# Hybrid encoder trunk on one core: w_out's first half loaded in pairs, some sums moved into the down-projection, x added sooner, sample's attention drawn in at other steps

## The chip, the cores and the metric

The kernel runs on one core of one Trainium2 chip. The metric is the device time of one launch in microseconds. The kernel before takes 1517.93 us, the median of three runs (1512.95 to 1520.29). Engines are named as in the profile: PE is TensorE, DVE VectorE, ACT ScalarE, POOL GpSimd, SP SyncE, which issues nearly all DMAs.

## The reference

One layer of an encoder trunk is run on two requests with shared weights: `x_prompt` (512 rows) and `x_sample` (1024 rows), each row 1024 wide, all float32.

```
def _trunk(x, ...):
    h = _rmsnorm(x, norm_attn_g);  z = h @ w_in                # 1024 -> 1792
    q, k, v, ca, cb = split(z)                                 # 8 heads, 2 kv heads, 512 conv channels
    a_out = _window_attn(q, k, v, bias, band, attn_sink)       # |q-k| <= 128, sink logit
    c = _dwconv(ca * sigmoid(cb), conv_dw_w, conv_dw_b)        # 31 taps
    c = silu(_layernorm(c, conv_ln_g, conv_ln_b))
    x = x + concat([a_out, c]) @ w_out                         # 1024 -> 1024
    h = _rmsnorm(x, norm_ffn_g)
    u = _dwconv(h @ w_up, ffn_dw_w, ffn_dw_b)                  # 1024 -> 5632, 3 taps
    x = x + (silu(u[:, :2816]) * u[:, 2816:]) @ w_down         # 2816 -> 1024
    return _rmsnorm(x, norm_final_g)
```

## The kernel before, in words

**Arithmetic.** Each float32 operand is split into a high part (a rounding copy on ACT) and a low part (a subtraction on POOL or DVE), and each product takes three matmuls: high by high, high by low, low by high. A usual matmul is 128x128 by 128x512. The large products of sample are done in blocks by Strassen's scheme in Winograd's form, seven products in place of eight, with sums and differences of blocks made beforehand.

**Tiles and slots.** SBUF is cut into slots by hand: 15 of 4096 bytes ("q"), 4 of 4352 ("c"), 61 of 2048 ("h"), 2 of 2304 ("d") and small ones. `sb.tile` takes the least slot that fits. PSUM banks are named a, u, b, c, later w (two banks wide) and t.

**Order.** The program's text is a plain sequence with Python generators drawn into it. `side` is a queue of generators, and `tick()`, called between matmuls, advances the first of them by `pace["rate"]` steps; `drain` runs a queue to its end. The text sets a priority. The build then orders the instructions of each engine by a simulated timeline, so a later instruction that is ready can go ahead of one that is not. In the last part (`by_hand`) PE keeps the order of the text, and in the down-projection SP does too. Each engine then runs its own list in order.

**Stages.**

1. The projection by w_in, chunk by chunk (L500, L289). In the later chunks the prompt's windowed attention runs as side work (`prompt_attention`).
2. `prompt_out`: w_out of the prompt. For each half `n` of its columns the eight chunks of 128 rows are loaded and split, and four blocks of 128 rows go through `out_half` (L770 to L772, 24 matmuls, a step after each 6). Then `make_h2` scales the rows by their norm and transposes them (L248): eight steps, each with four transposes, a scaled high part on ACT (L250) and a low part on DVE (L251). In front of it stand, for each block, the evacuation on DVE (L775), a sum of squares on ACT (L781), the power -1/2 on POOL (L138, L139) and the scaling on DVE (L828). A `while out` loop counts these steps in `n`, some 50 in all (2 x (1 + 4 + 16) + 8, if nothing has to be waited for). From step 19 on, every fourth (`SA` = 4) also takes one unit of sample's attention, `units_of_sample`: scores (L624, L628, L637), then values (L666, L668, L680, L690).
3. The prompt's up-projection and gate, 22 calls of `ffn_step`, each with 8 ticks at a rate of 0.55. The side work is `sample()`: the remaining units of sample's attention, then a wait for step 21 (`KW`), then loads of w_out's sixteen pieces of 128x512 (`load_wo`, L791, 256 KB each) with their splits (`split_wo`, L802 on ACT, L803 on DVE for two of four (`DW2` = 2) and on POOL for the others), then the conv norm of blocks 4 and 5 (`conv_norm`: transposes L729, statistics, L738, transposes L744, ACT, and the low part L754). Convolution steps of sample run as `late` work (L317, L318). At the end `drain(side)` puts all that is left into the text.
4. w_out of sample, blocks 4 to 11, through `out_blocks`, in the order (4,0), (4,1), (5,0), (5,1), ...: block, half.
5. Turning of rows into operands (L1079), then sample's up-projection: 22 steps `j`, each with seven products (`first` to `seventh`, L1148 to L1150). L1219 and L1237 are ACT's copies that seed a PSUM bank for the next product of a step. The prompt's gates are stored in DRAM, and `sums_of(p)` makes the sums that Winograd's form needs of them: two loads of 256 KB, four POOL steps (L966 to L969), two stores of 256 KB. There are eleven `p`; one is made at each even `j` from 2, and the last at `j` = 18.
6. The down-projection of both requests: 77 steps (i, p), seven products `i` in the order 1, 2, 5, 6, 7, 4, 3 with eleven `p` each (L1477 to L1479). `down_step(k)` loads (`load_next`), makes the operands of step k + 4 (`LEAD`; `operands` and `split_of`, L1036 and L1032 for the pairs, L1460 and L1032 for the prompt's part), and issues 12 or 18 matmuls. `evacuate` adds a finished product to the sums u, e, o11, o12 (L1029). `load_x1` and `with_x` load the residual x and add it to a sum (L1029 too, one of three parts on DVE, two on POOL).
7. The last product, i = 3, in a loop of its own over eleven `p`. Beside it, six blocks of rows that are complete are finished: `finish` sums squares on ACT (L1526), takes the power on POOL (L1548, L1549), scales on DVE (L1559) and on ACT and POOL (L1555, L1557) and stores. The last two groups of rows come at the end.

## Time and profile before

| what | value |
|---|---|
| median of three runs | 1517.93 us (1512.95 to 1520.29) |
| the profiled execution's own time | 1514.8 us |
| its span, first to last instruction | 1513.0 us |
| granted clock, mean | 0.992 |
| DMA over the span | 228.19 MB, mean 151 GB/s |
| w_out's matmuls (L770), prompt and sample | 280.4 to 744.0 us |
| prompt's and sample's w_in and the prompt's up-projection (L289) | 42.5 to 636.6 us |
| sample's up-projection (L1148) | 744.7 to 1191.6 us |
| down-projection (L1477) | 1178.2 to 1506.3 us |

Times in the profile are counted from the span's start. A row of a timeline gives start and duration in us, the engine, the line, the operation, what it writes and reads by the tiles' slot letters, its shape and count, and in brackets how long the engine was idle before it and what ended that. A row of the waits gives the total in us, how often, and the longest. A group's row gives busy us, the mean ns of one, and the engine's idle time in front. "PEclk" is the share of full speed that TensorE's clock was granted. Ends of matmuls are modelled, so pipelined matmuls overlap in the rows; the distance of their starts is what one costs.

### The profile page before, as it was taken

What the parts mean: (1) busy time and instruction counts of PE and PEld (TensorE: products, weight loads), DVE (VectorE), ACT (ScalarE), POOL (GpSimd) and SP (SyncE); (2) the same over time, 40 slices, a digit from 0 to 9 for tenths busy, and PEclk for the clock granted to TensorE, in tenths of its full rate; (3) what the DMA queues carried; (4) which work ended last, traced back from release to release, by engine and by line L of the source; (5) the groups of instructions that cost most, each with busy time, mean ns of one, the idle gap of its engine ahead of it and who ended that gap; (6) DMA issues with size and microseconds to landing.
All of it is one profiled execution on the core that took longest, in us unless ns stands there. A gap on an engine that the chain in (4) does not pass through costs nothing. (4 is left out here: it accounts for less than half of the span.)

```text
span 1513.0 us, 19880 instructions
## 1 busy us (share of the span) xinstructions
PE 1480.5 (98%) x6736; PEld 1216.5 (80%) x6736; DVE 1106.2 (73%) x1508; ACT 801.7 (53%) x1421; POOL 785.1 (52%) x691
## 2 busy tenths in 40 slices
PE   8999999999999999999999999999999999999997
PEld 7888788877888888778788788888888888888876
DVE  7877945648999895665767888888776855657865
ACT  6424455467777876653464445444454453443345
POOL 3454353356987875342436566565565211215666
PEclk9999999999999999999999999999999999999998
DMA  9455241843443444763124333333343473446744
GB/s 372 168 162 150 85 108 36 252 145 126 147 129 129 132 139 136 260 203 99 70 73 151 132 133 126 127 126 130 129 151 123 164 272 102 133 151 213 236 155 162
DMA packets 125201, 228.19 MB, mean 151 GB/s; under 512 B 20483, under 2 KB 45827, under 8 KB 124972
## 3 DMA queue, kind: packets, MB, share of 16 engines
q1 hardware_dynamic: 123564, 225.32, 45.4%
q10 hardware_dynamic: 1536, 1.61, 0.3%
q8 instruction: 53, 0.87, 0.2%
q14 instruction: 48, 0.39, 0.1%
HBM read 166.83 MB, written 61.10 MB: 151 GB/s over the span
## 5 line engine op out<-in xcount | busy, mean ns | idle before, releaser
L155 POOL TENSOR_TENSOR q<-q,q 128x1024 fp32r<-128x1024 f32 x66 | 158.6, 2406 | 76.2 <-ACT q L154 58.4
L1032 DVE TENSOR_TENSOR h<-h,h 128x512 fp32r<-128x512 f32 (+1 forms) x155 | 134.3, 891 | 82.9 <-ACT h L1036 36.4
L1032 POOL TENSOR_TENSOR q<-q,q 128x512 fp32r<-128x512 f32 x81 | 117.1, 1455 | 116.4 <-ACT q L1134 116.4
L1477 PE MATMUL w<-h,h 128*128 128x512 f32 x444 | 173.7, 391 | 1.3 <-ACT h L1460 0.8
L1479 PE MATMUL w<-h,h 128*128 128x512 f32 x436 | 170.1, 390 | 0.0
L1478 PE MATMUL w<-h,h 128*128 128x512 f32 x428 | 167.4, 391 | 2.8 <-DVE h L1032 2.8
L289 PE MATMUL u<-h,q 128*128 128x512 f32 x384 | 151.2, 395 | 0.3 <-DVE h L251 0.3
L291 PE MATMUL u<-h,q 128*128 128x512 f32 x384 | 150.4, 392 | 0.0
L290 PE MATMUL u<-h,q 128*128 128x512 f32 x384 | 150.2, 392 | 0.0
L1148 PE MATMUL w<-h,q 128*128 128x512 f32 x368 | 143.9, 391 | 2.9 <-ACT w L1237 2.6
L1150 PE MATMUL w<-h,q 128*128 128x512 f32 x368 | 143.7, 391 | 0.0
L1149 PE MATMUL w<-h,q 128*128 128x512 f32 x347 | 135.5, 390 | 0.0
L1032 POOL TENSOR_TENSOR h<-h,h 128x512 fp32r<-128x512 f32 (+1 forms) x36 | 48.5, 1348 | 161.9 <-ACT h L1460 109.6
L1036 ACT CAST h<-h 128x512 fp32r<-128x512 f32 x119 | 71.4, 620 | 109.3 <-DVE h L1032 43.6
L1477 PEld LDWEIGHTS w<-h,h 128*128 128x128 f32 x444 | 83.8, 189 | 19.7 <-ACT h L1460 1.2
L154 ACT CAST q<-q 128x1024 fp32r<-128x1024 f32 x66 | 69.1, 1049 | 54.5 <-PE u L290 31.1
L326 DVE SCALAR_TENSOR_TENSOR c<-d,cvw,c 128x512 f32<-128x512 f32 x128 | 95.9, 749 | 1.6
L1478 PEld LDWEIGHTS w<-h,h 128*128 128x128 f32 x428 | 80.7, 189 | 20.0 <-DVE h L1032 3.4
L1479 PEld LDWEIGHTS w<-h,h 128*128 128x128 f32 x436 | 82.1, 188 | 17.1
L1032 POOL TENSOR_TENSOR c<-q,c 128x512 fp32r<-128x512 f32 x46 | 72.5, 1586 | 41.8 <-ACT c L1134 41.8
L318 POOL TENSOR_TENSOR h<-h,h 128x512 f32<-128x512 f32 x62 | 80.5, 1300 | 17.9 <-ACT h L317 15.7
L1148 PEld LDWEIGHTS w<-h,q 128*128 128x128 f32 x368 | 69.1, 188 | 18.6 <-ACT w L1237 3.0
(455 smaller groups left out, 4010.9 us busy)
## 6 DMA issues: line engine op xcount, KB each, us to landing
q<-in_laid_w_up SPq DMA_DIRECT2D x88, 512.0 KB, 3.8
ga<-q SPq DMA_DIRECT2D x65, 256.0 KB, 2.2
h<-gap SPq DMA_DIRECT2D x57, 256.0 KB, 3.5
h<-ga SPq DMA_DIRECT2D x57, 256.0 KB, 3.2
h<-in_w_down SPq DMA_DIRECT2D x52, 256.0 KB, 3.3
q<-in_laid_w_in SPq DMA_DIRECT2D x22, 512.0 KB, 3.9
gap<-h SPq DMA_DIRECT2D x44, 256.0 KB, 2.8
q<-in_x_sample SPq DMA_DIRECT2D x15, 512.0 KB, 7.1
```

Of the source, the lines that this page charges most:

```text
L155: (nc.vector if dve else nc.gpsimd).tensor_tensor(lo[:], raw[:], hi[:].bitcast(F32), op=ALU.subtract)
L289: nc.tensor.matmul(out, whi[:, kc, :], hi[:], start=(kc == 0), stop=False)
L290: nc.tensor.matmul(out, whi[:, kc, :], lo[:], start=False, stop=False)
L291: nc.tensor.matmul(out, wlo[:, kc, :], hi[:], start=False, stop=(kc == KC - 1))
L326: nc.vector.scalar_tensor_tensor(acc[:], src(t), w(t), acc[:], op0=ALU.mult, op1=ALU.add)
L1032: (eng or nc.vector).tensor_tensor(out, a, b, op=ALU.subtract)
L1148: nc.tensor.matmul(out, whi[:, s], hi[:], start=(start and c == 0), stop=False, **go)
L1149: nc.tensor.matmul(out, whi[:, s], lo[:], start=False, stop=False, **go)
L1150: nc.tensor.matmul(out, wlo[:, s], hi[:], start=False, stop=(stop and c == 3), **go)
L1477: nc.tensor.matmul(out, sh[:, c], th[:], start=(p == 0 and not seeded), stop=False, **go)
L1478: nc.tensor.matmul(out, sh[:, c], tl[:], start=False, stop=False, **go)
L1479: nc.tensor.matmul(out, sl[:, c], th[:], start=False, stop=(p == NPAIR - 1), **go)
```

## The change

Seven things are changed.

- **Attention in the prompt's out-projection:** a unit of sample's attention is taken at every third step (`SA` = 3) while `n` is below 40 (`N2`), and at none of the later steps that occur (`SA2` = 99).
- **w_out of sample:** once step 16 (`KL`) of the prompt's up-projection is reached, the next unit of attention also issues the loads of the eight pieces of half 0, as four transfers of two pieces each. The wait for step 21 is gone. After the attention, the pieces of half 1 are loaded while half 0 is split; then comes the norm of block 4, then the splits of half 1, and after the last of them (`WN` = 7) the norm of block 5. Three of four low parts go to DVE (`DW2` = 3).
- **Order of the blocks:** the `drain` at the end of the prompt's up-projection is gone; the order is (4,0), (5,0), (4,1), (5,1), then as before, and each entry first advances the side work until its norm and its half of w_out are there.
- **Sums:** `sums_of` became a generator with stops between its steps, and its first store moved up two POOL steps. Sums 0 to 7 are made at `j` = 4, 6, ..., 18; sums 8, 9, 10 are drawn, one stop a step, into the down-projection from its step 2 on, ahead of that step's loads.
- **x:** the load of x for o12 moves from step 6 to step 4 of product 4; x is added to u at step 10, ahead of that product's evacuation, where before it was added behind it; all these steps now stand ahead of the evacuation.
- **Lead:** operands are made up to two steps further ahead from step 62 of the down-projection on, and six ahead (`LZ`), not four, in the last product, which also issues three loads a step (`LN`), not two.
- **Slots:** in the last product the two parts of a split share one q slot where one is free.

```diff
@@
 SCB, SCD = "aapa", "aaap"
-WOP, WOA, DW, DW2 = 1, 5, 2, 2
+WOP, WOA, DW, DW2 = 1, 5, 2, 3
 NE = 2
 YN = 2
 OB = "cbu"
 NW = 16
 BL = 9
-SA = 4
+SA, N2, SA2 = 3, 40, 99
+KL, WN = 16, 7
+LN = 3
+SUM_AT = (4, 6, 8, 10, 12, 14, 16, 18)
+XP = (2, 4, 4, 8, 8, 10)
+LZ = 6
 AP = 1
-KW = 21
 class Slots:
@@
         n += 1
         if n > 7:
             next(doubling, None)
-        if n % SA == 0 and n > 18:
+        if n > 18 and n % (SA if n < N2 else SA2) == 0:
             next(units_of_sample)
     drain(convs)
@@
         e, t, x, y = (sb.tile([2, HT]) for _ in range(4))
         nc.sync.dma_start(e[:], gap[1, 8][:, p])
         nc.sync.dma_start(t[:], gap[2, 4][:, p])
+        yield
         eng = nc.gpsimd
         eng.tensor_tensor(x[:, 1, :], e[:, 1, :], t[:, 1, :], op=ALU.add)
+        yield
         eng.tensor_tensor(x[:, 0, :], e[:, 0, :], e[:, 1, :], op=ALU.subtract)
+        nc.sync.dma_start(gap[7, 5][:, p], x[:])
+        yield
         eng.tensor_tensor(y[:, 0, :], x[:, 1, :], e[:, 0, :], op=ALU.subtract)
+        yield
         eng.tensor_tensor(y[:, 1, :], t[:, 0, :], y[:, 0, :], op=ALU.subtract)
-        nc.sync.dma_start(gap[7, 5][:, p], x[:])
         nc.sync.dma_start(gap[6, 3][:, p], y[:])
     def ffn_step(k):
@@
     want_up_raw(1, 0)
     at = [0]
+    fit = set()
+
+    def fitted(i):
+        yield from conv_norm(i)
+        fit.add(i)
+
     def sample():
-        yield from units_of_sample
-        while at[0] < KW:
+        for _ in units_of_sample:
             yield 0.0
+            if at[0] >= KL and not wor:
+                for kc in range(0, KC, 2):
+                    load_wo_pair(kc, 0)
         kt.clear(), vt.clear(), qt.clear(), bias.clear()
         use.update(norm="a")
         pace.update(rate=RN)
-        for m in range(16 + WOA):
-            if m in (10, 12):
-                load_cat(m // 2 - 1)
-            if m < 16:
-                load_wo(m // 2, m % 2)
-            if m >= WOA:
-                split_wo((m - WOA) // 2, m % 2, m % 4 < DW2)
-                yield 0.0
+        load_cat(4)
+        for kc in range(KC):
+            load_wo(kc, 1)
+            split_wo(kc, 0, kc % 4 < DW2)
+            yield 0.0
         drain(late)
-        for m in range(NE):
-            yield from conv_norm(4 + m)
+        yield from fitted(4)
+        for kc in range(KC):
+            if kc == 2:
+                load_cat(5)
+            split_wo(kc, 1, kc % 4 < DW2)
+            yield 0.0
+            if kc == WN:
+                yield from fitted(5)
     pace.update(rate=RD, late=CD)
     for k in range(NJ):
@@
     h2.clear()
     use.update(out=OB, turn="u")
     pace.update(rate=RE)
-    drain(side)
@@
     def sub(out, a, b, eng=None):
         (eng or nc.vector).tensor_tensor(out, a, b, op=ALU.subtract)
-    def split_of(src, dve=False):
-        hi, lo = sb.tile([NT], F32R), sb.tile([NT], F32R)
+    def split_of(src, dve=False, joint=False):
+        if joint and any(f[0][0] == "q" for f in sb.free):
+            both = sb.tile([2, NT], F32R, among="q")
+            hi, lo = Part(both, 0), Part(both, 1)
+        else:
+            hi, lo = sb.tile([NT], F32R), sb.tile([NT], F32R)
         nc.scalar.copy(hi[:], src)
         sub(lo[:], src, hi[:].bitcast(F32), None if dve else nc.gpsimd)
         return hi, lo
@@
         if n == 1:
             scaled(i)
-    for i in range(4, NB - 2):
-        if i + NE < NB:
-            side.appendleft(conv_norm(i + NE))
-        if i == 8:
+    turns_out = [(4, 0), (5, 0), (4, 1), (5, 1)] + [(i, n) for i in range(6, NB - 2) for n in range(2)]
+    for i, n in turns_out:
+        if n == 0:
+            (side.append if i < 8 else side.appendleft)(fitted(i + NE))
+        if (i, n) == (8, 0):
             side.append(turned(1, old_bank))
-        for n in range(2):
-            out_blocks(i, n)
+        while not (i in fit and (KC - 1, n) in wo):
+            advance(side)
+        out_blocks(i, n)
     reserve(4)
     for j in range(2):
         for half in range(2):
@@
             sub(b[:], b[:], pr.pop((B12, p))[:])
         else:
             b = pr.pop((B22, p))
-        hl[i, p] = (split_of(a[:], True), split_of(b[:], True))
+        joint = i == ORDER[-1]
+        hl[i, p] = (split_of(a[:], True, joint), split_of(b[:], True, joint))
         if p % 2 == 0:
             n = min(2, NPAIR - p) * HT
             raw = pr.pop((("p", i, 0), p))
@@
             made += 1
     pd = []
+    summed = deque(range(NPAIR))
+    rest = chain(*(sums_of(p) for p in range(len(SUM_AT), NPAIR)))
     def down_step(k):
         i, p = steps[k]
+        if k > 1:
+            next(rest, None)
         load_next(8 if k == 0 else 3 if len(pr) < CAP else 0)
-        make(k + (LEAD if k else 1))
+        make(k + (LEAD + max(0, min(2, (k - 60) // 2)) if k else 1))
         if p == 0:
             pd.extend(wide() for _ in range(2))
         hold = 5 if i == ORDER[0] else HOLD
@@
                 for tt in (4, 5):
                     mm_down(pd[2][:, (tt % 2) * NT:(tt % 2 + 1) * NT], i, q, tt)
                 hl.pop((i, q)), hp.pop((i, q))
+        if i == 7 and p == 4:
+            load_x1(0, 0)
+        if i == 7 and p == 8:
+            with_x("o11", 0, 0)
+        if i == 4 and p == XP[0]:
+            load_x1(1, 1)
+            fins.append(sb.tile([D]))
+            nc.sync.dma_start(fins[0][:], norm_final_g.partition_broadcast(P))
+            nc.scalar.activation(fins[0][:], fins[0][:], AF.Identity, scale=D ** 0.5)
+        if i == 4 and p == XP[1]:
+            with_x("e", 1, 1)
+        if i == 4 and p == XP[2]:
+            load_x1(0, 1)
+        if i == 4 and p == XP[3]:
+            with_x("o12", 0, 1)
+        if i == 4 and p == XP[4]:
+            load_x1(1, 0)
+        if i == 4 and p == XP[5]:
+            with_x("u", 1, 0)
         if p == NPAIR - 1:
             evacuate(i, pd)
             while pd:
                 pd.pop(0)
-        if i == 7 and p == 4:
-            load_x1(0, 0)
-        if i == 7 and p == 8:
-            with_x("o11", 0, 0)
-        if i == 4 and p == 2:
-            load_x1(1, 1)
-            fins.append(sb.tile([D]))
-            nc.sync.dma_start(fins[0][:], norm_final_g.partition_broadcast(P))
-            nc.scalar.activation(fins[0][:], fins[0][:], AF.Identity, scale=D ** 0.5)
-        if i == 4 and p == 4:
-            with_x("e", 1, 1)
-        if i == 4 and p == 6:
-            load_x1(0, 1)
-        if i == 4 and p == 8:
-            with_x("o12", 0, 1)
-            load_x1(1, 0)
     for j in range(2, NJ):
         for half in range(2):
@@
         if j >= NJ - 2:
             load_next(4)
         split_up(j + 1, 1, 2)
-        if (j - 2) // 2 < NPAIR and j % 2 == 0:
-            sums_of((j - 2) // 2)
-        if j == NJ - 4:
-            sums_of(NPAIR - 1)
+        if j in SUM_AT:
+            for _ in sums_of(summed.popleft()):
+                pass
         second(j)
         sums_up(j + 1)
         sixth(j)
@@
     for k in range(1, len(steps) - NPAIR):
         down_step(k)
-    with_x("u", 1, 0)
     u, e, o11, o12 = (acc.pop(n) for n in ("u", "e", "o11", "o12"))
     cut = lambda t, tt: t[tt // 2][:, (tt % 2) * NT:(tt % 2 + 1) * NT]
     base = len(steps) - NPAIR
@@
     z = wide()
     OTHER = {1: 2, 3: 3, 4: 8, 6: 9, 8: 10, 9: 11}
     for p in range(NPAIR):
-        load_next(2)
-        make(base + p + 4)
+        load_next(LN)
+        make(base + p + LZ)
         for tt in (0, 1):
             mm_down(z[:, tt * NT:(tt + 1) * NT], 3, p, tt)
         if p == HOLD:
```

## The prediction

> **What bounds the kernel now.** I read the head of the page first: how much of the span TensorE works.
>
> ```profile
> span 1513.0 us, 19880 instructions
> PE 1480.5 (98%) x6736; PEld 1216.5 (80%) x6736; DVE 1106.2 (73%) x1508; ACT 801.7 (53%) x1421; POOL 785.1 (52%) x691
> ```
>
> TensorE is the bound: 1513.0 - 1480.5 = 32.5 us of the span are all that it idles, and the change takes no matmul away. So only those idle times, and what they drag behind them, can be won. Second came the list of what TensorE waited for; its longest rows and one more:
>
> ```profile
> PE w L1478 <- DVE h L1032: 2.8, 1, 2.8
> PE w L1148 <- ACT w L1237: 2.6, 1, 2.6
> ...
> PE b L771 <- POOL h L803: 2.2, 1, 2.2
> PE w L1479 <- POOL d L1032: 1.6, 1, 1.6
> ...
> PE c L248 <- DVE q L828: 1.4, 1, 1.4
> PE a L680 <- ACT h L668: 1.4, 1, 1.4
> ...
> PE u L770 <- DMA h<-catd: 0.9, 1, 0.9
> ...
> PE w L1477 <- ACT h L1460: 0.8, 1, 0.8
> PE a L666 <- DVE s L628: 0.8, 1, 0.8
> ...
> PE b L770 <- ACT h L802: 0.3, 1, 0.3
> ```
>
> All single waits, in four places: L1477 to L1479 (the last down product), L1148 (the up products), L770/L771 (w_out of sample, where its halves are first used), L248/L666/L680 (the prompt's projection handing over to its up-projection). Third, the sums by stretch of those places. Columns: start:end, us, then busy us and count of PE, PEld, DVE, ACT, POOL, then granted clock, DMA share, GB/s.
>
> ```profile
> 328.30:342.90 14.60, 11.53 (x60) 8.69 (x58) 10.70 (x24) 11.96 (x26) 12.68 (x13) 0.88 0.22 75
> 336.10:339.50 3.40, 3.13 (x13) 2.94 (x14) 2.18 (x6) 2.62 (x6) 3.40 (x3) 0.50 0.54 154
> 639.00:657.00 18.00, 14.64 (x60) 10.68 (x61) 14.00 (x21) 12.06 (x24) 14.24 (x14) 0.91 0.85 311
> 653.60:657.00 3.40, 3.25 (x8) 2.60 (x9) 2.76 (x3) 0.15 (x1) 3.40 (x5) 0.50 0.12 43
> 1472.00:1483.00 11.00, 5.85 (x16) 3.90 (x16) 8.61 (x6) 7.23 (x18) 8.98 (x10) 0.69 0.25 95
> 1476.20:1483.00 6.80, 4.03 (x10) 2.75 (x9) 5.58 (x4) 4.04 (x11) 4.78 (x5) 0.50 0.30 116
> 550.00:575.00 25.00, 25.00 (x121) 20.85 (x121) 21.37 (x38) 17.57 (x32) 18.40 (x17) 1.00 0.41 138
> 1200.00:1225.00 25.00, 25.00 (x112) 20.71 (x112) 16.57 (x21) 12.20 (x21) 4.82 (x4) 1.00 0.83 298
> ```
>
> In each of the three first places a stretch at half clock (0.50) follows the idle time. What that costs is read from the timeline of TensorE behind the 2.25 us wait:
>
> ```profile
> 653.75 0.80 PE L771 MATMUL b<-h,h 128*128 128x512 f32 x1 [2.25 <-POOL h L803]
> ...
> 656.05 0.63 PE L770 MATMUL b<-h,h 128*128 128x512 f32 x1
> 656.48 0.63 PE L771 MATMUL b<-h,h 128*128 128x512 f32 x1
> ...
> 657.18 0.39 PE L771 MATMUL u<-h,h 128*128 128x512 f32 x1
> 657.41 0.40 PE L772 MATMUL u<-h,h 128*128 128x512 f32 x1
> ```
>
> At half clock a matmul starts 0.43 us after the one before, at full clock 0.23. So a place costs its idle time plus half of the busy time at half clock. Hand-over of the projection: 14.60 - 11.53 = 3.1 idle, 3.13 / 2 = 1.6, together 4.7; the two waits of L680 and L666 behind it (1.4 + 0.8) make 6.9. w_out of sample: 18.00 - 14.64 = 3.4, and 3.25 / 2 = 1.6: 5.0. Last product: 11.00 - 5.85 = 5.2, and 4.03 / 2 = 2.0: 7.2. That is 19.1 us in reach of the edits.
>
> The Trainium skill ("TensorE: Matmul & The Clock Gate", section on HAM oscillation) warns of idle gaps above about 3.4 us alone; by it none of these gaps would cost clock, and a place would be worth its idle time only. The rows above show half clock behind a gap of 2.25 us, so the trace decides and the clock share is counted. By the page the three places would be worth 5.2 us less, and the sum made below 9.4 us instead of 13.0.
>
> **The last down product (LZ, LN, LEAD, XP, joint).** Nothing is added but order. Three waits, 0.8 + 1.6 + 2.8 = 5.2 us, end on ACT, POOL and DVE splits of operands. Why these are late:
>
> ```profile
> 1472.07 1.76 DVE L1559 SCALAR_TENSOR_TENSOR q<-q,s,c 128x512 f32<-128x512 f32 x1 [1.77 <-POOL s L1549]
> ...
> 1477.78 4.04 DVE L1032 TENSOR_TENSOR h<-h,h 128x512 fp32r<-128x512 f32 x3
> ```
>
> DVE sat 1.77 us in front of a finishing step (L1559) that waits for POOL's power (L1549), with the splits (L1032) queued behind it. The change makes operands two steps earlier, so they stand ahead of these finishing steps in every queue. Two steps of 12 matmuls are 2 x 12 x 0.23 = 5.5 us, more than the longest wait (2.8). And x is added to u before the fourth product lands, where it now comes after:
>
> ```profile
> 1459.02 3.30 POOL L1029 TENSOR_TENSOR q<-q,q 128x1024 f32<-128x1024 f32 x1 [3.50 <-DVE q L1029]
> ...
> 1465.17 2.84 POOL L1029 TENSOR_TENSOR q<-q,q 128x1024 f32<-128x1024 f32 x1
> ```
>
> These two POOL adds end at 1468.0; issued before the evacuation they leave POOL's queue free for the power of the first finishing steps some 6 us sooner. Six 256 KB loads of x move two steps up SP's queue and gain cover. Three waits and the clock go: 7.2; I leave 1.0 for a finishing step that now ends nearer the last matmul. **Win 6.2**, bounds 0 (finishing steps hold the queues as now) and 7.2. PE and SP are ordered by hand here, so this edit is the surest.
>
> **w_out of sample (pairs, order of blocks, DW2, KL, WN).** Four loads of two chunks replace eight in a row, 2.1 MB, issued in or after step 16 of the prompt's up-projection; 550 to 575 shows that stage with DMA at 0.41 and no idle TensorE, which hides them. Today:
>
> ```profile
> h<-in_laid_w_out SPq DMA_DIRECT2D x12, 256.0 KB, 4.8
> ...
> L802 ACT CAST h<-h 128x512 fp32r<-128x512 f32 x16 | 9.3, 622 | 3.7 <-DMA h<-catd 1.6 <-DMA h<-in_laid_w_out 1.6 <-PE a L681 0.4
> ...
> L803 POOL TENSOR_TENSOR h<-h,h 128x512 fp32r<-128x512 f32 x8 | 11.5, 1449 | 8.3 <-PE a L680 6.5 <-ACT h L802 1.6
> ```
>
> Twelve of the sixteen chunks are issued between 620 and 655 (first row), against DMA at 0.85, and all sixteen splits precede the first block in the text. After, eight do, and of sixteen low parts POOL makes four, not eight: 4 x 1.45 = 5.8 us off POOL, whose L803 is the releaser of the 2.2 us wait. That wait, the 0.3 on L802 and the clock's 1.6 go: 4.1. The 0.9 on catd stays. Sample's attention leaves one unit more to this place: its 108 units (16 x 2 of scores, 76 of values) meet 7 calls in the projection (steps 21 to 39) instead of 8 (20 to 48), and 22 x 8 x 0.55 = 97 in the up-projection; I charge 0.3. Waiting for step 21 (KW) goes, at nothing: attention outlasts it. **Win 3.8**, bounds 5.0 and the loss of a rival below.
>
> **Sample's attention in the prompt's projection (SA, N2).** Calls every third step up to 39 fall among the out-projection's matmuls, where today's every fourth makes TensorE wait for nothing. The steps from 40 on, the last block and the turning of the rows, get none. The chain there:
>
> ```profile
> 328.97 0.67 DVE L775 TENSOR_TENSOR q<-u,q 128x512 f32<-128x512 f32 x1
> ...
> 334.55 1.76 DVE L828 TENSOR_SCALAR q<-q,rs 128x1024 f32<-128x1024 f32 x1 [0.90 <-POOL rs L139]
> ```
>
> ```profile
> 332.35 0.19 POOL L138 TENSOR_SCALAR rs<-s 128x1 f32<-128x1 f32 x1
> 332.62 1.26 POOL L318 TENSOR_TENSOR h<-h,h 128x512 f32<-128x512 f32 x1
> ```
>
> From the evacuation's start to the last scaling's end, 328.97 + 7.34 = 336.31, 7.3 us pass; the scaling itself (L828) could run as soon as POOL has its power, and POOL does convolution adds (L318, 1.26) between, which stay. Against that, attention fills TensorE in this chain now. Bounds: win all 6.9; or lose 4.2 (a bare chain: 7.3 idle + 1.6 clock = 8.9 against 4.7). The program's order here is chosen at build, which may pull attention of the up-projection in as filler. I take **3.0**, nearer the win, since that attention is ready and only stands later in the text.
>
> **Sums.** One sum is four POOL steps:
>
> ```profile
> L967 POOL TENSOR_TENSOR h<-h 128x256 f32<-128x256 f32 x11 | 11.1, 1010 | 8.7 <-DVE w L1029 8.7
> L969 POOL TENSOR_TENSOR h<-h,h 128x256 f32<-128x256 f32 x11 | 9.7, 881 | 0.8
> ```
>
> About 4 x 0.9 = 3.6 us; three sums move from the up products into down steps 2 to 14, 11 us of POOL, which works 4.82 of 25 us there. Their twelve transfers of 256 KB are 3.1 MB; at the 298 GB/s of 1200 to 1225, 10.6 us of a DMA at 0.83. Operands are made 4 steps ahead (4 x 12 x 0.23 = 11 us), so I take 0; uncovered, up to 10.6 are lost. SP's writes wait for POOL ahead of the next loads; same cover. The 2.6 us wait on L1237 lies in up step 3, and a sum still stands at step 4, as now: 0, though 2.6 could go.
>
> **Sum.** 6.2 + 3.8 + 3.0 = 13.0. The profiled execution took 1514.8 us (span 1513.0 and 1.8 around it), 3.1 under the median of the three runs, 1517.93; it would become 1501.8, and the median 1504.9. I forecast **1505**. About 0.5%, 7.6 us, is what a measurement of this kernel can tell from no change: faster is below 1510.3, slower above 1525.5.
>
> **Rivals.**
> *The clock does not come back.* Waits that are left over still end in half-clock stretches, so only idle time is won: 13.0 less 3.6, the clock's 5.2 in the share won (13.0 of 19.1), is 9.4: 1508.5. Against it stand the three 0.50 rows, each right behind its gap. Chance 0.10, faster. The page of the Trainium skill named above comes to the same time by another way: gaps as short as these would cost no clock, so their closing would return none.
> *It doesn't do what it says.* Outside the hand-ordered parts the build sets the order: if splits and attention run where they run now, only the last product gains: 1517.9 - 6.2 = 1511.7. For it: the L248 and L770 places are not hand-ordered. Chance 0.13, same.
> *The bare chain.* The hand-over's chain runs without any filler: 4.2 lost for 3.0 won, 13.0 - 7.2 = 5.8, 1512.1. For it: nothing of the projection is left to run in those 7.3 us. Against it: today's filler came from the same stock of attention. Chance 0.09, same.
> *Block 5 starves (slower).* Block 5's norm now stands behind all sixteen splits, and its first half waits for it.
>
> ```profile
> 641.14 0.55 PE L729 MATMUL a<-ident,h 128*128 128x128 f32 x3
> ```
>
> ```profile
> 655.58 1.66 DVE L754 TENSOR_TENSOR h<-h,h 128x512 fp32r<-128x512 f32 x1
> ```
>
> A norm takes 641.14 to 657.24, 16.1 us; behind 16 casts of 0.62, 26.0. TensorE has block 4's first half and half of block 5's without it, 36 x 0.23 = 8.3. Idle 17.7 + clock 1.7 = 19.4, against 5.0: 14.4 lost, 1517.9 - 6.2 - 3.0 + 14.4 = 1523.1. It decides when that norm ends more than 8.3 us behind block 4's start and the second half's splits are late too; if these come, 36 more matmuls fill another 8.3. Chance 0.15: 0.08 past 1525.5 (with the bare chain too, 1530.3), 0.07 same.
>
> **Numbers.** The forecast gets 0.53. Faster 0.53 + 0.10 = 0.63, same 0.13 + 0.09 + 0.07 = 0.29, slower 0.08. Low end: all 19.1 and the 2.6 won, 1496. High end: the forecast with the 10.6 us of transfers uncovered, 1515.5, so 1516; it holds all but the starving block.
>
> **What would show it.** Right: no wait of L1477 to L1479 above 0.5 us and no half clock before the last matmuls; no wait on L803; L289's first matmul closer behind the projection's last L772 than today; the two POOL adds of x ahead of the fourth product's evacuation. The 2.6 us on L1237 still there. Wrong: waits at the first steps of the down products on DMA; a long wait of L770 on the norm (L754); TensorE idle over 5 us before L248.

## The result and the profile after

The kernel after takes 1511.51 us, median of 20 runs (1509.03 to 1515.45), against 1516.39 for the kernel before (20 runs, 1512.95 to 1520.29): a ratio of 0.9973 (95% interval 0.9965 to 0.9981), 0.27% or 4.1 us faster. The forecast was 13.0 us. The interval leaves out 1, so the difference is real, but it is smaller than the 0.5% that the prediction named as the least that can be told from no change.

Lines moved in the code: the last products' matmuls L1477–L1479 are L1502–L1504 in the kernel after, the adds L1029 are L1047, the splits L1032 are L1050, the low parts of w_out L803 are L807, the copy L1237 is L1261, the projection's matmuls L289–L291 are L293–L295, the transposes L248 are L252, and the convolution step on DVE ahead of the prompt's gates is L939.

Head of the page of the kernel after:

```profile
span 1512.6 us, 19879 instructions
PE 1480.4 (98%) x6736; PEld 1218.5 (81%) x6736; DVE 1127.4 (75%) x1512; ACT 801.5 (53%) x1421; POOL 778.8 (51%) x687
```

This execution took 1514.4 us, 2.9 above its median; the profiled execution of before lay 1.6 below the median of its 20 runs. So the two spans, 0.4 us apart, say nothing of the gain; what is read below are places. The four splits that the change moved to DVE show: 1508 instructions became 1512 there, 691 became 687 on POOL.

What TensorE waited for in the kernel after, the rows that answer to those of before:

```profile
PE w L1502 <- DVE q L1047: 7.2, 2, 6.2
PE u L293 <- DVE h L939: 3.0, 2, 2.2
...
PE c L252 <- DVE q L832: 1.2, 1, 1.2
...
PE u L775 <- DVE h L807: 1.0, 1, 1.0
...
PE w L1170 <- ACT w L1261: 0.9, 1, 0.9
...
PE b L774 <- DMA h<-catd: 0.2, 1, 0.2
```

The three waits of the last product (2.8, 1.6, 0.8) are gone, and so is the 2.2 us on POOL's low parts of w_out. The 2.6 us on the copy L1237 is 0.9. But a single wait of 6.2 us is new and longer than the three together: the last product's first matmul waits for L1047 on DVE, which is the evacuation of product 4. The new product writes a PSUM bank (w) that this evacuation has to read first. A second new wait, 2.2 us on L939, lies in the prompt's up-projection.

The same stretches as before, and two at the new wait (start:end, us, busy us and count of PE, PEld, DVE, ACT, POOL, granted clock, DMA share, GB/s):

```profile
1454.50:1467.70 13.20, 7.03 (x22) 5.32 (x21) 13.20 (x12) 6.14 (x12) 6.81 (x4) 0.74 0.14 50
1460.90:1467.70 6.80, 4.74 (x11) 3.77 (x12) 6.80 (x9) 3.49 (x7) 1.28 (x1) 0.50 0.12 47
639.00:657.00 18.00, 15.46 (x73) 11.58 (x72) 15.12 (x24) 12.92 (x25) 8.43 (x8) 1.00 0.87 302
328.30:342.90 14.60, 12.42 (x68) 10.05 (x67) 9.17 (x20) 13.31 (x27) 9.98 (x9) 0.88 0.25 87
```

At w_out of sample TensorE is busy 15.46 of 18.00 us at full clock, where it was 14.64 at 0.91. At the hand-over of the projection the clock is where it was (0.88). At the last product the idle time is 13.20 - 7.03 = 6.2 us and the clock costs 4.74 / 2 = 2.4 more: 8.6, where before it was 7.2.

**Why the evacuation came late.** Timeline of DVE in the kernel after (start, us, engine, line; in brackets the idle time in front). Product 4's last matmul starts at 1456.40:

```profile
1449.77 1.23 DVE L1047 TENSOR_TENSOR q<-q,q 128x1024 f32<-128x1024 f32 x1 [0.65 <-DMA q<-x1d]
1450.91 0.69 DVE L1050 TENSOR_TENSOR h<-h,h 128x512 fp32r<-128x512 f32 x1
1451.74 2.67 DVE L1050 TENSOR_TENSOR q<-h,q 128x512 fp32r<-128x512 f32 x1
1454.34 4.57 DVE L1050 TENSOR_TENSOR h<-h,h 128x512 fp32r<-128x512 f32 x2
1458.83 1.74 DVE L1050 TENSOR_TENSOR q<-h,q 128x512 fp32r<-128x512 f32 x1
1460.49 1.28 DVE L1050 TENSOR_TENSOR h<-h,h 128x512 fp32r<-128x512 f32 x2
1461.70 1.21 DVE L1047 TENSOR_TENSOR q<-w,q 128x1024 f32<-128x1024 f32 x1
```

POOL at that time:

```profile
1451.27 2.59 POOL L1047 TENSOR_TENSOR q<-q,q 128x1024 f32<-128x1024 f32 x1 [2.70 <-DMA q<-x1d]
1453.83 2.86 POOL L1047 TENSOR_TENSOR q<-q,c 128x1024 f32<-128x1024 f32 x1
1456.63 1.73 POOL L1050 TENSOR_TENSOR d<-h,h 128x512 fp32r<-128x512 f32 x1
1458.32 1.70 POOL L1050 TENSOR_TENSOR h<-h,h 128x512 fp32r<-128x512 f32 x1
```

And TensorE:

```profile
1456.40 0.39 PE L1504 MATMUL w<-h,h 128*128 128x512 f32 x1
1462.96 0.80 PE L1502 MATMUL w<-h,h 128*128 128x512 f32 x1 [6.17 <-DVE q L1047]
```

A split on DVE that takes 0.69 us at 1450.91 takes 2.67 at 1451.74, where POOL began its add of x at 1451.27. It ends at 1454.41, 0.55 us behind POOL's 1453.86: it stood until POOL was done. From 1451.74 to 1461.70 six splits take 9.96 us; at the pace of the last two (1460.49 to 1461.70, 0.60 each) they would take 3.6. The 6.3 us lost are about the 6.2 us that TensorE waits. Of them 4.2 us fall on the two splits beside POOL's adds of x (1451.74 to 1457.16, 5.4 us), and 2.1 us on the next two, which run beside POOL's own splits (L1050 at 1456.63 and 1458.32): these too read two SBUF tiles. Behind its first row DVE lists no idle time here, so only the durations tell of it.

The Trainium skill ("SBUF — State Buffer", section on who interferes with whom) says that a DVE instruction with two inputs in SBUF and a GpSimd instruction that reads SBUF exclude each other for the whole instruction: the later one stands until the other is done. The rows agree: both operations read two SBUF tiles.

### The profile page after: what moved, and what is told of

It reads as the page before. It is cut to its first block, busy times and chain, and to the rows that moved or that the text cites. A ratio compares the mean times of both kernels' runs of the same rounds, so it can differ in the third digit from the quotient of the medians.

```text
span 1512.6 us, 19879 instructions
## 1 busy us (share of the span) xinstructions
PE 1480.4 (98%) x6736; PEld 1218.5 (81%) x6736; DVE 1127.4 (75%) x1512; ACT 801.5 (53%) x1421; POOL 778.8 (51%) x687
## 5 line engine op out<-in xcount | busy, mean ns | idle before, releaser
L1050 POOL TENSOR_TENSOR q<-q,q 128x512 fp32r<-128x512 f32 x81 | 117.1, 1454 | 128.5 <-ACT q L1156 128.5
L1050 DVE TENSOR_TENSOR h<-h,h 128x512 fp32r<-128x512 f32 (+1 forms) x153 | 130.9, 881 | 66.0 <-ACT h L1058 23.2
L1502 PE MATMUL w<-h,h 128*128 128x512 f32 x436 | 170.8, 392 | 7.2 <-DVE q L1047 7.2
L1504 PE MATMUL w<-h,h 128*128 128x512 f32 x432 | 168.8, 391 | 0.0
L293 PE MATMUL u<-h,q 128*128 128x512 f32 x384 | 152.0, 396 | 3.0 <-DVE h L939 3.0
L295 PE MATMUL u<-h,q 128*128 128x512 f32 x384 | 150.9, 393 | 0.0
L1050 POOL TENSOR_TENSOR h<-h,h 128x512 fp32r<-128x512 f32 (+1 forms) x38 | 52.1, 1372 | 150.0 <-ACT h L1485 108.2
L1502 PEld LDWEIGHTS w<-h,h 128*128 128x128 f32 x436 | 82.4, 189 | 25.3 <-DVE q L1047 8.1
L1504 PEld LDWEIGHTS w<-h,h 128*128 128x128 f32 x432 | 81.7, 189 | 17.2
L1050 POOL TENSOR_TENSOR c<-q,c 128x512 fp32r<-128x512 f32 x46 | 75.1, 1642 | 36.6 <-ACT c L1156 36.5
L293 PEld LDWEIGHTS u<-h,q 128*128 128x128 f32 x384 | 72.5, 189 | 17.7 <-ACT h L318 2.4
```

The source lines that it names most:

```text
L293: nc.tensor.matmul(out, whi[:, kc, :], hi[:], start=(kc == 0), stop=False)
L295: nc.tensor.matmul(out, wlo[:, kc, :], hi[:], start=False, stop=(kc == KC - 1))
L1050: (eng or nc.vector).tensor_tensor(out, a, b, op=ALU.subtract)
L1502: nc.tensor.matmul(out, sh[:, c], th[:], start=(p == 0 and not seeded), stop=False, **go)
L1504: nc.tensor.matmul(out, sl[:, c], th[:], start=False, stop=(p == NPAIR - 1), **go)
```

## The experiments

Each kernel below "after" has 5 to 12 runs, spread over three chips, on which the kernel before has medians from 1515.5 to 1517.5 us. So ratios are compared, not medians; each ratio is to the kernel before on the same chip. Microseconds are the ratio less 1, times 1517.

| kernel | median us | ratio (95% interval) | us |
|---|---|---|---|
| after (all edits) | 1511.51 | 0.9973 (0.9965–0.9981) | -4.1 |
| last product alone | 1514.58 | 0.9989 (0.9979–0.9999) | -1.7 |
| w_out alone | 1512.81 | 0.9973 (0.9963–0.9982) | -4.1 |
| attention alone | 1518.22 | 1.0017 (1.0004–1.0030) | +2.6 |
| sums alone | 1513.52 | 0.9977 (0.9966–0.9987) | -3.5 |
| all but attention | 1507.78 | 0.9948 (0.9935–0.9962) | -7.9 |
| the same, x late | 1504.14 | 0.9922 (0.9909–0.9934) | -11.8 |
| the same (x early), short lead | 1511.17 | 0.9970 (0.9958–0.9982) | -4.6 |
| the same (x early), x on DVE | 1507.16 | 0.9942 (0.9928–0.9956) | -8.8 |
| all, x late | 1504.64 | 0.9930 (0.9917–0.9943) | -10.6 |
| all, x late, late calls kept | 1507.05 | 0.9950 (0.9934–0.9966) | -7.6 |
| all, x late, every fourth to step 40 | 1505.38 | 0.9933 (0.9920–0.9946) | -10.2 |
| last product alone, x late | 1510.72 | 0.9961 (0.9946–0.9976) | -5.9 |

Their lines are shifted again: matmuls of the down products L1537–L1539 (a line more in some), adds L1073 or L1074, splits L1076 or L1077, the copy L1237 is L1296 or L1297, and L939 is L941 or L942. The diffs are shortened to the lines that matter.

### The four parts, each alone

Each kernel is the one before with one part of the change. *The last product's edit alone* (x, lead and slots together):

```diff
-LZ, LN = 4, 2;  XP = (2, 4, 6, 8, 8, behind the evacuation)
+LZ, LN = 6, 3;  XP = (2, 4, 4, 8, 8, 10)
-        make(k + (LEAD if k else 1))
+        make(k + (LEAD + max(0, min(2, (k - 60) // 2)) if k else 1))
```

> The kernel before with the edit of the last down product alone (x sooner, operands made further ahead, split pairs in one slot). Theory A, the cover moved: the splits that now stand ahead and the early adds of x on POOL keep DVE from the evacuation of product 4, so the three waits (0.8, 1.6, 2.8 us) give way to one of about 6 us at the first matmul of the last product, half clock behind it as before, and the time is within 2 us of before. Theory B, the edit wins what was forecast and something else in the full change eats it: no wait above 0.5 us in this place, and about 6 us less than before.

Measured: 0.9989, 1.7 us won. Its longest wait:

```profile
PE w L1537 <- DVE q L1073: 6.2, 1, 6.2
```

The wait on the evacuation belongs to this edit and comes without the others.

*w_out's edit alone* (pairs, order of the blocks, `DW2` = 3, no `drain`):

```diff
-WOP, WOA, DW, DW2 = 1, 5, 2, 2
+WOP, WOA, DW, DW2 = 1, 5, 2, 3
+            if at[0] >= KL and not wor:
+                for kc in range(0, KC, 2):
+                    load_wo_pair(kc, 0)
-    drain(side)
+    turns_out = [(4, 0), (5, 0), (4, 1), (5, 1)] + ...
```

> The kernel before with the edit of sample's w_out alone (pairs, order of blocks, three of four low parts on DVE). Theory A: the 2.2 us wait on a POOL split and the half clock behind it go, some 2 us of small waits stay: 3 to 4 us less than before, nearly all that the full change wins. Theory B, the gain of the full change comes from a sum of small moves elsewhere: 0 to 1.5 us less.

Measured: 0.9973, 4.1 us won. Its stretch at w_out:

```profile
639.00:657.00 18.00, 16.22 (x79) 12.41 (x78) 14.20 (x24) 10.37 (x21) 7.95 (x9) 1.00 0.74 251
```

Idle 18.00 - 16.22 = 1.8 us against 3.4 before, and full clock: 1.6 + 1.6 of the 4.1 us lie in this stretch. Block 5 does not starve.

*Attention's edit alone:*

```diff
-        if n % SA == 0 and n > 18:                      # SA = 4
+        if n > 18 and n % (SA if n < N2 else SA2) == 0:  # 3, 40, 99
```

> The kernel before with sample's attention drawn in at every third step up to 39 and not after, alone. Theory A: the build fills the chain in front of the transposes with attention from the up-projection all the same, so the waits stay about as they are, 0 to 2 us to either side of before. Theory B, the edit wins by itself (3 us less) and the other edits cost that again.

Measured: 1.0017, 2.6 us lost (0.6 to 4.6): no gain, and a little more lost than the theory expected. Its profiled execution took 1525.8 us, the slowest of its twelve, so its waits are not read here.

*The sums' edit alone:*

```diff
-        if (j - 2) // 2 < NPAIR and j % 2 == 0:
-            sums_of((j - 2) // 2)
+        if j in SUM_AT:                                  # 4, 6, ..., 18
+            for _ in sums_of(summed.popleft()):
+                pass
+        if k > 1:                                        # in down_step
+            next(rest, None)
```

> The kernel before with the sums moved alone. Theory A: one sum less stands ahead of up step 4, the wait on L1237 shrinks from 2.6 to under 1 us, and no wait is added in the down-projection: 1 to 2.5 us less. Theory B, as forecast: a sum stands at step 4 as before, the wait stays, 0 us; or the transfers that are moved into the first down steps make TensorE wait there, up to 10 us more.

Measured: 0.9977, 3.5 us won. The wait of 2.6 us on the copy L1237 does not occur in this kernel, and no new wait appears in the down products. It is 1.9 us with the last product's edit alone and 2.4 with w_out's, which keep the old sums. Where the two kernels part can be read from DVE, here first in the kernel before: the store of step 2's sum holds it, and later it waits for POOL ahead of the copy.

```profile
797.78 0.69 DVE L1032 TENSOR_TENSOR h<-q 128x512 f32<-128x512 f32 x1 [0.93 <-DMA gap<-h]
831.72 1.79 DVE L1032 TENSOR_TENSOR h<-q 128x512 f32<-128x512 f32 x1 [3.72 <-POOL q L1032]
```

With the sums' edit the first of these waits is missing, and the second is short:

```profile
827.81 0.98 DVE L1076 TENSOR_TENSOR h<-q 128x512 f32<-128x512 f32 x1 [0.78 <-POOL q L1076]
```

The sum of step 4, which the prediction had in mind, runs on POOL in both kernels (from 817.55 and from 814.17).

### What holds the evacuation

Four kernels follow. All have the change without attention's edit; the first has only that. Theory: x's early adds on POOL block DVE's splits, and with them the evacuation queued behind. Rival: the longer lead, with more splits ahead of the evacuation, is what makes it late.

```diff
-SA, N2, SA2 = 3, 40, 99
+SA, N2, SA2 = 4, 999, 4
```

> The full change without its attention edit (every fourth step to the end, as before). Theory A, the edits act nearly by themselves: w_out, sums and last product give about -4, -3.5 and -2 us, the attention edit costs 2 to 3, so this is 7 to 10 us below before and 2 to 4 below the full change. Theory B, the gaps shift with any change of order and the single figures don't add: no faster than the full change (4 to 5 us below before).

Measured: 0.9948, 7.9 us won, as the theory expected. The wait on the evacuation is 4.8 us here.

*x behind the evacuation, as before:*

```diff
-        if i == 4 and p == XP[5]:
-            with_x("u", 1, 0)
...
     for k in range(1, len(steps) - NPAIR):
         down_step(k)
+    with_x("u", 1, 0)
```

> The kernel noattn, with x added to u behind product 4's evacuation, as before; operands still six steps ahead. Theory A, the wait of 6 us at the last product's start comes from POOL's two adds of x, which slow DVE's splits in front of the evacuation: it falls below 2 us and the time by 4 to 6 us. Theory B, it comes from the splits that are made further ahead: it stays above 4 us, and the time stays within 1.5 us.

Measured: 0.9922, 11.8 us won, 3.9 more than with early x; the two intervals do not meet. It is the lowest ratio of all. Timeline of DVE:

```profile
1450.96 1.21 DVE L1074 TENSOR_TENSOR q<-w,q 128x1024 f32<-128x1024 f32 x1
1452.10 0.68 DVE L1077 TENSOR_TENSOR h<-h,h 128x512 fp32r<-128x512 f32 x1
1452.70 1.21 DVE L1074 TENSOR_TENSOR q<-w,q 128x1024 f32<-128x1024 f32 x1
1453.83 1.21 DVE L1074 TENSOR_TENSOR q<-q,q 128x1024 f32<-128x1024 f32 x1
1454.96 2.89 DVE L1077 TENSOR_TENSOR h<-h,h 128x512 fp32r<-128x512 f32 x1
```

and TensorE's busy time in the last product, 40.00 of 40.00 us at full clock:

```profile
1440.00:1480.00 40.00, 40.00 (x178) 33.12 (x177) 30.15 (x30) 25.36 (x60) 25.00 (x30) 1.00 0.32 109
```

The split beside POOL's add is as slow as ever (2.89), but two pieces of the evacuation, the ones that read the bank, stand ahead of it, and TensorE doesn't wait for it.

*The old lead, x early* (the joint slots stay):

```diff
-LZ, LN = 6, 3
+LZ, LN = 4, 2
-        make(k + (LEAD + max(0, min(2, (k - 60) // 2)) if k else 1))
+        make(k + (LEAD if k else 1))
```

> The kernel noattn, with operands made four steps ahead as before, two loads a step in the last product; x still added before the evacuation. Theory A (POOL's adds slow DVE): a wait of 3 us or more on the evacuation stays, and late splits make TensorE wait later in the last product as well; not faster than noattn. Theory B (lead): no wait on the evacuation above 1 us, the three waits of before come back at about 5 us, time within 2 us of noattn.

Measured: 0.9970, and the wait on the evacuation is 8.4 us, longer than with the long lead. Timeline of DVE:

```profile
1447.78 1.22 DVE L1073 TENSOR_TENSOR q<-q,q 128x1024 f32<-128x1024 f32 x1 [5.14 <-DMA q<-x1d]
1448.92 3.48 DVE L1076 TENSOR_TENSOR h<-h,h 128x512 fp32r<-128x512 f32 x2
1452.33 2.87 DVE L1076 TENSOR_TENSOR q<-h,q 128x512 fp32r<-128x512 f32 x1
```

So the rival falls: the wait stays without the longer lead. Splits beside POOL's adds are slow here too (2.87). A second mechanism shows: at its early place the add stands in DVE's queue before x has come, and DVE is idle for 5.14 us with the splits queued behind it (0.65 in the kernel after).

*All three adds of x to u on DVE:*

```diff
-            add(..., x[w][:], nc.gpsimd if w else None)
+            add(..., x[w][:], nc.gpsimd if w and name != "u" else None)
```

> The kernel noattn, with all three adds of x to u on DVE instead of one on DVE and two on POOL. Theory A (POOL's adds slow DVE's splits): DVE's splits in front of the evacuation take 0.7 us each again, the wait falls to 0 to 3 us although DVE itself gets 2.4 us more work, and the time falls by 3 to 6 us. Theory B (lead): DVE has yet more in front of the evacuation, so the wait grows to 7 us or more.

Measured: 0.9942, not told apart from 0.9948 by time, so the 3 to 6 us that the theory expected did not show. The wait halves, to 2.4 us, and most splits around the adds are quick again:

```profile
1444.92 0.68 DVE L1076 TENSOR_TENSOR h<-h,h 128x512 fp32r<-128x512 f32 x1
1445.52 0.69 DVE L1076 TENSOR_TENSOR q<-h,q 128x512 fp32r<-128x512 f32 x1
1446.13 0.68 DVE L1076 TENSOR_TENSOR h<-h,h 128x512 fp32r<-128x512 f32 x1
1446.73 1.22 DVE L1073 TENSOR_TENSOR q<-q,c 128x1024 f32<-128x1024 f32 x1
```

DVE pays for the adds with 2 x 1.2 us of its own, and the next splits run beside POOL's own splits (1.78 us for the one at 1447.86); that some wait is left fits both.

### Late x with the full change, and where attention loses

> The full change, with x added to u behind the fourth product's evacuation as in the kernel before. Theory: the early adds of x and attention's edit are two separate losses that add. Attention alone cost 2.6 us, and 3.7 us within the full change (1511.5 against 1507.8 without it), so this lands 2.6 to 3.7 us above the kernel without attention's edit and with late x (1504.1): a ratio of 0.994 to 0.995 to the kernel before, no wait at the start of the last product, and the 2.2 us wait on a convolution step near 358 us still there. Rival: attention's edit cost only through the last product's queues: then 1504, a ratio of 0.992.

The edit is that of the first x-late kernel, on the full change. Measured: 0.9930, 10.6 us won, 6.5 more than by the change as it was made. That lies between what the theory (0.994 to 0.995) and the rival (0.992) expected, and its interval overlaps with that of the kernel without attention's edit (0.9909 to 0.9934): by these two ratios attention's edit costs 1.2 us with late x, but their intervals leave room for 0 and for the full 3.7. Whether the two losses add is not decided. The wait on L939 (L942 here), 2.2 us, is there.

```diff
-SA, N2, SA2 = 3, 40, 99
+SA, N2, SA2 = 3, 40, 4
```

> As the full change with late x, but sample's attention goes on at every fourth step in the projection's last steps (ten calls instead of seven; eight before). Theory: what costs is that the last steps get none, since the hand-over to the up-projection then finds more attention left to run in its chain: here the loss of 2.6 to 3.7 us goes, 0.992, or below. Rival: drawing it every third step costs, because it fills the vector engines' queues ahead of the last block: then 0.994 to 0.995 as in the full change with late x.

Measured: 0.9950 (0.9934 to 0.9966), if anything slower. The loss did not go when the late calls came back, so the theory is not borne out. In its trace the long wait of that stretch is another, 2.8 us on L675.

```diff
-SA, N2, SA2 = 3, 40, 99
+SA, N2, SA2 = 4, 40, 99
```

> As the full change with late x, but attention at every fourth step up to step 40, then none (five calls). Theory: the missing calls in the last steps cost: 0.994 to 0.995, or more, as three units more are left for the up-projection. Rival (every third step is what costs): 0.992.

Measured: 0.9933. The three kernels overlap with each other; neither half of the edit can be named as the cause.

### The last product's edit alone, x late

Its edit is the first diff of the experiments with the one that puts `with_x("u", 1, 0)` behind the evacuation. The longer lead, the joint slots and the sooner load of x for o12 are left.

> The kernel before with the last product's edit alone, but x added to u behind the fourth product's evacuation as before: only the longer lead of the operands and the joint tiles are left of the edit. Theory (x's early adds ate the gain of the longer lead): no wait above 0.5 us and no half clock in the last product, and the priced win of 5.2 us of idle time and 2.0 of clock less the finishing steps, 6.2 in all: a ratio near 0.996, against 0.9989 with the early adds. Rival (the lead wins nothing by itself, and the gain of late x within the full change comes by its meeting other edits): 0.998 or above, with waits of the last product or the finishing steps behind it in the list.

Measured: 0.9961, 5.9 us won (3.6 to 8.2) where the same edit with early x wins 1.7. TensorE in the last product:

```profile
1440.00:1480.00 40.00, 40.00 (x178) 33.15 (x177) 32.51 (x31) 23.25 (x51) 22.21 (x21) 1.00 0.37 123
```

No idle time and full clock. The theory holds, and its number lies within the interval. The profiled executions show the two terms of that number. The table gives the stretch from the first to the last start of the first of the three matmul lines of the down products (L1477 before), and what is left of the span behind it.

| kernel | down products, us | us behind them |
|---|---|---|
| before | 1178.2 to 1506.3: 328.1 | 6.7 |
| last product alone | 1176.1 to 1504.9: 328.8 | 6.8 |
| last product alone, x late | 1180.1 to 1500.9: 320.8 | 9.0 |
| all but attention | 1172.6 to 1500.4: 327.8 | 6.8 |
| the same, x late | 1173.5 to 1493.3: 319.8 | 10.3 |
| the same (x early), short lead | 1173.3 to 1504.8: 331.5 | 6.7 |
| the same (x early), x on DVE | 1171.4 to 1496.0: 324.6 | 6.8 |

Late x shortens the stage by 8.0 us in both pairs, and the finishing steps behind it give 2.2 and 3.5 us of that back.

## Why the prediction was wrong, and where it was right

**Last down product, 6.2: the step that failed is "issued before the evacuation they leave POOL's queue free".** The prediction looked at the queue from which the two adds go and not at the engine beside which they now run. The step was not needed either: with late x POOL's power steps behind the adds start no sooner (L1589 at 1472.10 in the last product's edit alone, L1528 at 1467.98 before), and TensorE is busy throughout 1440 to 1480. The rest of the edit does what was priced: 5.9 us measured against 6.2, and by the table 328.1 - 320.8 = 7.3 us of stage against 7.2. The 1.0 us left for the finishing steps was too little, 9.0 - 6.7 = 2.3. The early adds take 4.2 of that back alone (5.9 - 1.7), and 6.5 in the full change (10.6 - 4.1). The trace of before had the row that shows it. Timeline of DVE in the kernel before, beside POOL's add at 1459.02 of 3.30 us that the prediction quotes:

```profile
1458.87 1.21 DVE L1029 TENSOR_TENSOR q<-q,q 128x1024 f32<-128x1024 f32 x1
1460.00 2.88 DVE L1032 TENSOR_TENSOR h<-h,h 128x512 fp32r<-128x512 f32 x1
1462.80 1.21 DVE L1029 TENSOR_TENSOR q<-w,q 128x1024 f32<-128x1024 f32 x1
```

A split of 0.7 us takes 2.88, and one piece of the evacuation (L1029 reading w) stands behind it. Two adds ahead of the whole evacuation, by these rows 2 x 2.2 us of DVE, should have been charged; in the kernel after they take 4.2. Early adds of x ("the two POOL adds of x ahead of the fourth product's evacuation") were even listed as a sign that the prediction is right; they were the sign of the loss. Why the edit with early x still gains 1.7 us (0.2 to 3.2), though its stage is no shorter (328.8 against 328.1), is open.

**w_out of sample, 3.8: right.** 4.1 measured alone. L803's wait and the half clock went as said; some 0.7 to 1.0 us waits on splits and the rest on catd are left.

**Sample's attention, 3.0: wrong in sign.** It was taken nearer to the win, "since that attention is ready". In 328.30 to 342.90 TensorE's busy time did rise, from 11.53 to 12.42 us, 0.9 at the same clock of 0.88. The sign that the prediction named came too: L289's first matmul starts 12.7 us behind the projection's last L772 (329.86 to 342.57), where it was 14.9 (328.07 to 342.94), and the out-projection in front, from its first matmul to that one, is no longer (47.9 us from 282.0, 47.7 from 280.4 before). But behind the hand-over the two waits of 1.4 and 0.8 us (L680, L666) gave way to one of 2.2 us on L939, and the stretch's clock fell. Kernel before, and then after, from the hand-over to 375 us:

```profile
328.00:375.00 47.00, 41.72 (x199) 33.39 (x198) 39.03 (x68) 34.97 (x64) 32.45 (x27) 0.96 0.38 119
```

```profile
328.00:375.00 47.00, 42.16 (x197) 34.30 (x197) 39.81 (x70) 37.18 (x68) 37.45 (x30) 0.93 0.36 119
```

199 matmuls against 197: nothing is won here. The bound of -4.2 in the prediction was worked out for an idle chain; attention still runs in the chain, so that was not the cause either. So the step that failed is the price put on attention that "only stands later in the text": drawn in at other steps it shortens the hand-over by 2.2 us, and a wait of 2.2 us comes back 16 us behind it. Why that ends in a loss, 2.6 us alone and 3.8 in the full change (0.9973 against 0.9948), stays open. In the profiles sample's up-projection starts at 744.7 us with the edit in the full change and at 741.0 without it, 744.5 and 742.6 with late x; but four kernels whose text is alike up to there (before, last product alone with early and with late x, sums alone) start it between 743.4 and 745.6, so one profile of each can't price the edit. The wait on the evacuation is longer with it (6.2 against 4.8), though the order by hand is the same in both.

**Sums, 0: wrong by 3.5 us.** "The 2.6 us wait on L1237 lies in up step 3, and a sum still stands at step 4, as now" kept the wait because step 4 keeps its sum. The run shows that the edit of the sums takes the wait away, and the traces that step 4's sum was not enough to cause it, for it runs in both. What went is step 2's sum: its store held DVE at 797.78, and the matching rows of DVE, level before it (792.84 and 792.87), lie 1.9 us apart behind it (L1285 at 798.99, with the edit 797.12). That this lateness is the wait 36 us later is read from the rows, not tested, and the edit also moves a store. The prediction named the 2.6 as what could go and left it out of the sum. The cost that it feared, transfers in the down-projection, did not appear.

**Clock.** Its share came back where waits went: 1.00 at w_out (0.91 before), and 1.00 in the last product with late x. So the rival "The clock does not come back" is not what happened.

**The rivals.** "It doesn't do what it says" gives 1511.7, which is the time measured, by the opposite of its mechanism: w_out and the sums gained (4.1 and 3.5), and the edit ordered by hand, "the surest", gained 1.7. "The bare chain" gives 1512.1, as near, but the chain was not bare (12.42 of 14.60 us busy). Block 5 did not starve. The number alone would have borne out a wrong story.

**The sum, as measured.** With late x: -5.9 - 4.1 - 3.5 + 2.6 = -10.9, and the whole gives -10.6; with intervals of 1.4 to 2.3 us to either side of each term, so close a match is partly luck. With the edit as made: -1.7 - 4.1 - 3.5 + 2.6 = -6.7 against -4.1; the difference of 2.6 is within what the intervals of the four, each 1.4 to 2.0 to either side, leave open.

## What to carry to other kernels

When work moves ahead of a wait, ask which engine runs beside it at its new place and what is queued there for TensorE, not only whose queue becomes free. Look in the trace for rows of one form whose duration jumps, here from 0.7 to 2.7 us, and then at the neighbour in the same microseconds. The list of waits named the instruction that stood behind the slow ones (L1047), not their cause. An evacuation that frees a PSUM bank for the next product belongs ahead of what can wait in its queue; here that was worth 3.9 us and more.

## What the runs showed of the hardware

**Half clock behind short gaps comes and goes.** In the first projection all kernels have the same two gaps of TensorE, 1.1 and 1.3 us, which end near 156 to 158 and 159 to 160 us, and no edit touches them. The stretch around them in three executions, first the kernel before, then w_out's edit alone, then the last product's edit alone with late x:

```profile
157.00:163.80 6.80, 5.46 (x19) 4.27 (x20) 6.69 (x14) 3.18 (x7) 2.29 (x3) 0.75 0.20 78
```

```profile
157.00:163.80 6.80, 5.46 (x26) 4.42 (x27) 6.68 (x14) 3.21 (x8) 2.29 (x3) 1.00 0.20 78
```

```profile
157.00:163.80 6.80, 5.46 (x16) 4.18 (x15) 6.68 (x14) 3.34 (x8) 2.28 (x3) 0.54 0.20 78
```

The same busy time holds 19, 26 or 16 matmuls; between the ends lie 10 x 0.23 = 2.3 us, about a third of the spread of one kernel's runs (1509.0 to 1515.5). A gap's clock share, which the prediction counted in full, is thus not certain for gaps of this length (here part of the stretch ran at half clock, 0.54 to 0.78 in the mean, in eleven of the fourteen profiled executions), and one profile can't settle it. The Trainium skill ("TensorE: Matmul & The Clock Gate", section on what's actually happening) tells of a free-running window of about 3.4 us; the half-clock stretches at w_out and at the last product were 3.4 and 6.8 us long, which agrees, and a window whose phase differs from run to run would give rows like these three; the runs do not show that this is the cause. Its rule on gaps above 3.4 us does not cover gaps this short.
